# A hybrid gMLP and state-space block on one Trainium2 core: fixed places for the sums, the dt products and the modulation products of the first stage

## The chip, the cores and the metric

The kernel runs on one core of a Trainium2 chip. A core has five engines that run at the same time, each working through its own list of instructions in order: TensorE (PE in the profile) multiplies matrices, VectorE (DVE) and ScalarE (ACT) work element by element, GpSimd (POOL) does odd jobs, and SyncE (SP) mostly issues DMA transfers. An instruction that needs another engine's result waits on a semaphore, and everything behind it on its own engine waits with it. Operands lie in the on-chip memory SBUF, the results of matmuls in the accumulators of PSUM, which has eight banks; inputs and intermediate results too large for these lie in HBM.

The metric is the device time of one execution in microseconds (us), as the median of several runs. Lower is better.

## The reference, cut to what matters

One layer of a decoder trunk over a sequence of 1024 positions with width 1024. The first stage of the kernel computes `h` and its first products; the rest feeds on `h`.

```python
def hybrid_layer(x, c, ada_w, ada_b, norm_w, w_in, ...):
    mod = jax.nn.silu(c) @ ada_w + ada_b
    shift, scale, gate = jnp.split(mod, 3, axis=-1)
    h = rms_norm(x, norm_w) * (1 + scale[:, None, :]) + shift[:, None, :]
    proj = h @ w_in
    gm_u, gm_v, gm_z, ssm_z, xbc, dt_raw, g_a, g_b = jnp.split(proj, SPLITS, axis=-1)
    y_a = spatial_gating(gelu(gm_u), gelu(gm_v), gm_ln_w, gm_ln_b, gm_ws, gm_bs) * silu(gm_z)
    ...                       # causal convolution, state-space scan over 32 heads -> y_b
    merged = sigmoid(g_a) * (y_a @ w_proj_a) + sigmoid(g_b) * (y_b @ w_proj_b)
    return x + gate[:, None, :] * (merged @ w_out)

# reference(): x = hybrid_layer(x, c, ...); return rms_norm(x, final_norm_w)
```

`x` is 1024 x 1024, `w_in` is 1024 x 11296 and `ada_w` 1024 x 3072, all in float32.

## The kernel before, in words

The large products go through a scheme with seven products in place of eight: the 1024 x 1024 matrix `h`, transposed, is cut into quarters b11, b12 (upper row tiles, left and right half of the positions), b21 and b22 (lower row tiles), and besides b11, b21 and b22 the sums t1 to t4 of quarters are operands. To keep float32's accuracy with a faster matmul type, every operand is held as two parts, a rounded high part (written by ScalarE, `A.copy`) and the low part that is left (by VectorE, `V.tensor_sub`); a product then takes three matmuls: high by high, low by high, high by low.

The first stage makes all of this. Its loop runs over the eight row tiles of `h` (128 channels each) in the order `KS = (0, 4, 1, 5, 2, 6, 3, 7)`, so that a row tile k of the upper half and its partner k + 4 follow each other. With n as the place in this order, one row tile goes through these steps:

- SyncE loads a 1024 x 256 piece of `ada_w` (`load_aw`, two buffers, so the load for n + 2 waits for the product that reads n) and 128 x 256 of `w_in` (`load_w0`).
- `matvec(n)`: TensorE multiplies silu(c) by the piece of `ada_w`, eight matmuls into the bank `pm`; ScalarE copies the result to `row`.
- `modulation(n)`: two 128 x 1 matmuls turn the row into columns, again in `pm`, and VectorE makes the scale and shift `md` of the tile from them in two short instructions.
- `transposes(n, half)`: TensorE turns four 128 x 128 blocks of the already normed `x` into a bank `px`.
- `rows_of_h(n, half)`: from `px` and `md` ScalarE writes the rounded part and then the full value `hf`, and VectorE the low part. A tile has two halves, so four ScalarE instructions of 512 columns.
- `first_products(n)`: twelve matmuls, six for each half, add the tile's share of the first 256 gate columns into `acc`. Its generator gives the places, counted from 1 to 12, at which other work of the next tile is put: `prepare(n + 1)` holds what goes to which place.
- `dt_products(k)`: when both partners of k are there, four matmuls add their share of `dt_raw` into the bank `pd`. They read the full values `hf`.
- The sums: VectorE overwrites `hf` in four subtractions (the first makes b12 - b11 in the place of b11), which can only be done when `dt_products(k)` has read the values; then each of t1 to t4 is split into its two parts. For k = 0 to 2 this is `t_first`, `t_second`, `t_third` and `t_parts`; for k = 3 it is `last_sums` and what follows the stage.

Between these, at place 12 of tile n = 4, `small_parameters` transposes two blocks of small parameters into a bank `pp1` and VectorE copies them out in two instructions. `pp1` is allocated under the tag `pm`, which has one buffer: it is the bank that `matvec` and `modulation` use, and the next `matvec` may write there only when both copies are done. The diff does not touch `small_parameters`.

The order of instructions on an engine comes from a scheduler that sorts by its own estimate of when work is ready. An instruction wrapped in `pin` is held behind the instruction that the program wrote just before it on the same engine. A row of pinned instructions therefore keeps the program's order; an instruction without `pin` between them breaks the row, since it may itself go early or late, and what is pinned behind it is held behind nothing else. In the kernel before, matmuls and most work of the stage are pinned; the sums and splits of k = 0 to 2 are not. On VectorE the order that came out at tile n = 4 is: `md` of tile 5, the two copies of `small_parameters`, and then the low parts of tile 5's two halves, although the program writes the low parts first. Ahead of the loop, tiles n = 0 and the beginning of n = 1 are written out by hand, among `warm` matmuls that only keep TensorE running.

The first stage ends when the main stage's products begin (`vx` on line 944, whose first operand is `p1v0h`), and from there the kernel is one long row of matmuls with the other engines beside it.

Of the kernel before, what the change touches and what calls it, by code (L numbers as in the profile page):

```python
# [16 lines left out]
P = 128  # L17
D = 1024
S = 1024
KT = D // P  # L20
# [15 lines left out]
def hybrid_kernel(  # L36
# [131 lines left out]
    with tc.tile_pool(name="p0", bufs=1, reuse_waits="tile") as p0:  # L168
# [98 lines left out]

        def modulation(n):

            k, pm, row = KS[n], pms[n], mds[n]  # L270
            for j in range(2):
                mm(pm[:, 256 + j : 257 + j], row[:, j * P : (j + 1) * P], ones[:, 0:1])
# [33 lines left out]
        def t_split(nm, k, t):  # L306
            hi, lo = bop[nm][0][k], bop[nm][1][k]
            A.copy(hi, t)
            V.tensor_sub(lo, t, f32(hi))

        def t_first(k):

            b11, b12 = hfs[k, 0], hfs[k, 1]
            V.tensor_sub(b11, b12, b11)
            t_split("t1", k, b11)

        def t_second(k):

            b11, b12, b22 = hfs[k, 0], hfs[k, 1], hfs[k + 4, 1]
            V.tensor_sub(b12, b22, b12)  # L320
            V.tensor_sub(b22, b22, b11)

        def t_third(k):

            b21, b22 = hfs[k + 4, 0], hfs[k + 4, 1]
            V.tensor_sub(b21, b21, b22)
            t_split("t2", k, b22)

        def t_parts(k):

            t_split("t3", k, hfs[k, 1])
            t_split("t4", k, hfs[k + 4, 0])

        def last_sums(step):
            b11, b12, b21, b22 = hfs[3, 0], hfs[3, 1], hfs.get((7, 0)), hfs.get((7, 1))
            if step == 0:
                V.tensor_sub(b11, b12, b11)
# [62 lines left out]
        warm(2)  # L400
        modulation(0)
# [51 lines left out]
        sums = {(7, 9): [(last_sums, 0)], (7, 10): [(last_sums, 1)], (7, 11): [(last_sums, 2)]}  # L453
# [1469 lines left out]
```

## Time and profile before

| What | Value |
|---|---|
| Median of 3 runs | 1402.44 us (1399.79 to 1406.72) |
| The profiled execution's own time | 1400.27 us |
| Its span in the profile | 1398.5 us |
| Mean granted TensorE clock | 0.997 of full speed |
| First product of the main stage | 73.86 us from the span's start |

The profile shows one execution. Its views used below are: the page with busy time by engine and the chain of waits that ended last; windows, which give for stretches of time the busy time of each engine (with the number of instructions in brackets), the granted TensorE clock, the DMA share and GB/s; waits, which list who waited for whom; and the timeline, in which a row is the start and length of some merged instructions, their engine and line, what they write and read, how many, and in square brackets how long the engine had been idle before and what ended that. PEld is TensorE's loading of weights. A float32 matmul shows as two records, so eight matmuls of `matvec` are x16.

### The profile page before, as it was taken

Reading aid. Unit: us, or ns where it says so; the run is one execution under the profiler, and the core shown is the slowest. Engines: PE = TensorE matmul, PEld = TensorE weight load, DVE = VectorE, ACT = ScalarE, POOL = GpSimd, SP = SyncE. Lnnn points to the kernel's source line nnn. Section 1 sums busy time; section 2 is a strip of 40 time slices with the busy share of each in tenths; the row PEclk is TensorE's granted clock in tenths of the full one; section 3 lists DMA queues with packets and bytes.
Section 4 is the critical chain, followed back from the end, with each engine's and each line's share of the span. In section 5 each row is a group of like instructions: output and inputs, shape, how many; then the busy total and the mean of one; then the engine's idle time right before and its main releaser. Section 6 shows DMA issues by size and latency. Waiting matters only on the chain.

```text
span 1398.5 us, 20239 instructions
## 1 busy us (share of the span) xinstructions
PE 1366.6 (98%) x6959; PEld 1131.6 (81%) x6959; DVE 1047.8 (75%) x1701; ACT 800.1 (57%) x1447; POOL 221.7 (16%) x212
## 2 busy tenths in 40 slices
PE   7999999999999999999999999999999999999998
PEld 6678888888888888778888888888788888788886
DVE  4776876777778889688788786388777755859976
ACT  4754666666566665455666555587776713223453
POOL 1000000000000011121000110027778750000002
PEclk9999999999999999999999999999999999999999
DMA  9675443333334667686665775598778757978913
GB/s 266 172 244 143 141 120 116 103 121 113 121 121 147 199 192 242 217 255 204 215 199 169 237 235 151 174 349 308 270 257 289 254 184 248 351 252 318 369 69 121
DMA packets 247227, 288.60 MB, mean 206 GB/s; under 512 B 14508, under 2 KB 194132, under 8 KB 247124
## 3 DMA queue, kind: packets, MB, share of 16 engines
q1 hardware_dynamic: 173716, 203.76, 45.4%
q10 hardware_dynamic: 73408, 83.54, 17.5%
q8 instruction: 55, 0.90, 0.3%
q14 instruction: 48, 0.39, 0.1%
HBM read 199.79 MB, written 87.46 MB: 205 GB/s over the span
## 4 chain that ended last, share of the span: by engine, by line
PE 77%; DMA 8%; DVE 7%; ACT 3%; issue 3%; POOL 2%; SPq 1%; ACTq 0%; DVEq 0%; POOLq 0%
PE xuz L559 6%; PE xx L559 6%; PE xcb L559 5%; PE xz L559 5%; PE xg L559 4%; PE pma L81 3%; PE ox L1767 3%; DMA dcy<-acs_d 3%; PE yuz L559 3%; PE yp L1581 3%; PE vx L944 3%; PE yx L559 3%; PE ycb L559 3%; PE yz L559 3%; PE yg L559 2%
## 5 line engine op out<-in xcount | busy, mean ns | idle before, releaser
L782 POOL TENSOR_TENSOR wog<-wog,gb 128x256 f32<-128x256 f32 x16 | 21.6, 1366 | 628.3 <-DMA wog<-in_w_out_dram 604.1
L1102 ACT ACTIVATE dcy<-dcy,nacs 128x128 f32<-128x128 f32 x256 | 78.5, 388 | 15.2 <-POOL dcy L1097 15.1
L1097 POOL TENSOR_SCALAR_AFFINE_SELECT dcy<-dcy 128x1024 f32<-128x1024 f32 x32 | 35.4, 1107 | 137.2 <-ACT ea L1094 137.1
L1094 ACT ACTIVATE ea<-dcy 64x512 f32<-64x512 f32 x64 | 40.1, 626 | 12.4 <-DMA dcy<-acs_d 12.0
L1519 DVE SCALAR_TENSOR_TENSOR yn<-yn,par,rb 128x512 f32<-128x512 f32 x32 | 23.9, 747 | 27.0 <-DMA yn<-yb_d 26.9
L81 PE MATMUL pma<-yh,wah 128*128 128x512 f32 x128 | 43.3, 419 | 0.0
L81 PE MATMUL pma<-yh,wal 128*128 128x512 f32 x128 | 42.5, 413 | 0.0
L1122 DVE TENSOR_TENSOR dcy<-dcy,pc 128x1024 f32<-128x1024 f32 x32 | 38.9, 1216 | 4.7 <-PE pc L84 3.9
L1017 ACT ACTIVATE ac<-ac 128x1024 f32<-128x1024 f32 x32 | 33.9, 1061 | 13.6 <-DVE ac L1015 13.3
L1184 POOL TENSOR_TENSOR yz<-y,sl 128x512 f32<-128x512 f32 x32 | 41.5, 1296 | 1.1
L1182 DVE TENSOR_TENSOR ym<-yn,ea 128x512 f32<-128x512 f32 (+1 forms) x32 | 19.9, 622 | 28.7 <-PE yn L81 28.6
L81 PE MATMUL pma<-yl,wah 128*128 128x512 f32 x128 | 40.1, 394 | 0.0
L1183 POOL TENSOR_TENSOR y<-y,ym 128x512 f32<-128x512 f32 (+1 forms) x32 | 36.6, 1143 | 14.5 <-DVE ym L1182 14.0
L81 PEld LDWEIGHTS yn<-sl,st 128*128 128x128 f32 x224 | 30.7, 193 | 9.6 <-POOL yz L1184 3.6
L81 PE MATMUL yn<-sl,st 128*128 128x128 f32 x224 | 32.1, 279 | 6.1 <-DVE st L1152 6.1
L1782 POOL TENSOR_TENSOR r<-r,fnw 128x512 f32<-128x512 f32 x4 | 5.3, 1345 | 204.5 <-ACT junk L1780 204.5
L81 PE MATMUL sp<-xe,bn 128*128 128x256 f32 x112 | 32.6, 408 | 4.3 <-DVE ssq L1213 1.7
L814 ACT CAST wbb<-wbr 128x512 fp32r<-128x512 f32 x32 | 19.8, 620 | 28.8 <-DMA wb_d<-wbb 21.6
L1015 DVE SCALAR_TENSOR_TENSOR ac<-c2x,cwt,ac 128x1023 f32<-128x1023 f32 (+2 forms) x24 | 31.2, 1298 | 6.4 <-ACT ac L1013 6.3
L979 ACT ACTIVATE vm<-vm,vr 128x128 f32<-128x128 f32 x64 | 25.8, 483 | 16.2 <-DMA vm<-v_d 15.8
L1015 DVE SCALAR_TENSOR_TENSOR ac<-c2cb,cwt,ac 128x1023 f32<-128x1023 f32 (+2 forms) x24 | 31.2, 1299 | 5.2 <-ACT ac L1013 5.0
L81 PE MATMUL yi<-dcy,xd 128*64 128x128 f32 x512 | 35.0, 279 | 0.0
(2981 smaller groups left out, 4427.0 us busy)
## 6 DMA issues: line engine op xcount, KB each, us to landing
sl<-s_d SPq DMA_DIRECT2D x32, 768.0 KB
s_d<-ac ACTq DMA_DIRECT2D x32, 512.0 KB
wb_d<-wbb ACTq DMA_DIRECT2D x32, 512.0 KB
dcy<-acs_d SPq DMA_DIRECT2D x32, 512.0 KB
av<-in_w_in_dram SPq DMA_DIRECT2D x36, 256.0 KB
aw<-in_ada_w_dram SPq DMA_DIRECT2D x16, 512.0 KB
wbr<-in_w_proj_b_dram SPq DMA_DIRECT2D x32, 256.0 KB
yb_d<-yz ACTq DMA_DIRECT2D x32, 256.0 KB
```

Source lines behind the costliest of these rows:

```text
L81: pin(PE.matmul(acc, l, r, start=first, stop=last))
L559: pin(PE.matmul(ps, lw[:, k * P : (k + 1) * P], r[k], start=first and n + k == 0, stop=n == 2 and k == 3, skip_group_check=not first))
L944: pin(PE.matmul(ps[pn][j], l[:, j * P : (j + 1) * P], r, start=nm in ("p1", "p5", "p2") and n + units[i][1] == 0, stop=n == 2 and k == 3, ...
L1015: V.scalar_tensor_tensor(ac[:, s:], cc[:, : S - s], conv_wt[:, 3 - s, i : i + 1], ac[:, s:], op0=ALU.mult, op1=ALU.add)
L1094: A.activation(ea[hh * HD : (hh + 1) * HD], dcy.rearrange("p (j e) i l -> p e j (i l)", e=2)[hh * HD : (hh + 1) * HD, hh], AF.Exp)
L1097: G.affine_select(out=d8, in_=d8, compare_op=ALU.is_ge, fill=-1e30, base=0, pattern=[[0, 2 * HPG], [1, P]], channel_multiplier=-1)
L1102: A.activation(dcy[:, h, i, :], dcy[:, h, i, :], AF.Exp, bias=sub[:, i, h : h + 1])
L1122: V.tensor_tensor(d3, d3, pc[:, 0:256].unsqueeze(1).to_broadcast([P, HPG, 256]), op=ALU.mult)
L1183: G.tensor_add(y1[:, :, t0:], y1[:, :, t0:], m[:, :, t0:])
L1184: G.tensor_mul(yz, y1, sl[:, 4:6])
L1581: pin(PE.matmul(ps[j], a[:, v, js], r, start=first and n + k == 0, stop=n == 2 and k == KT - 1, skip_group_check=not first))
L1767: pin(PE.matmul(ps, a[:, tsl], b[:, cs], start=first and n + j == 0, stop=n == 2 and j == 3, skip_group_check=not first))
```

## The change

The diff moves work within the first stage. No computation is added or removed, except for four more `warm` matmuls.

- `modulation` is cut in two: `modulation_product` (the two 128 x 1 matmuls) and the two VectorE instructions. For tile 1 the written-out beginning now has the transposes and `rows_of_h(0, 1)` ahead of `matvec(1)`, and the product behind the first two matmuls of tile 0's second half; the split of `w_in`'s piece for tile 1 now stands ahead of VectorE's part of `modulation(1)`.
- The sums and splits of k = 0 to 2 are pinned and put at fixed places: `second` (the work at place 7, at place 8 for n = 2) and `between`.
- `dt_products` for k = 1 and 2 move from place 2 of the odd tile to the end of the transposes at place 7 of the same tile; for k = 3 from place 8 to place 6. `last_sums` for k = 3 moves from places 9, 10, 11 to 7, 8, 9, and its first sum is pinned.

```diff
-        def modulation(n):
-
-            k, pm, row = KS[n], pms[n], mds[n]
+        def modulation_product(n):
+
+            pm, row = pms[n], mds[n]
             for j in range(2):
                 mm(pm[:, 256 + j : 257 + j], row[:, j * P : (j + 1) * P], ones[:, 0:1])
+
+        def modulation(n):
+
+            k, pm = KS[n], pms[n]
             md = p0.tile([P, 2], F32, name=f"md{n}", tag="md", bufs=3)
...
         def t_split(nm, k, t):
             hi, lo = bop[nm][0][k], bop[nm][1][k]
-            A.copy(hi, t)
-            V.tensor_sub(lo, t, f32(hi))
...
+            pin(A.copy(hi, t))
+            pin(V.tensor_sub(lo, t, f32(hi)))
+
+        def t_sum(k, i):
+
+            b11, b12, b21, b22 = (hfs[k + 4 * (j // 2), j % 2] for j in range(4))
+            a, b, c = ((b11, b12, b11), (b12, b22, b12), (b22, b22, b11), (b21, b21, b22))[i]
+            pin(V.tensor_sub(a, b, c))
+
+        def t_part(k, nm):
+
+            t_split(nm, k, hfs[{"t1": (k, 0), "t3": (k, 1), "t2": (k + 4, 1), "t4": (k + 4, 0)}[nm]])
...
         start = first_products(0)
         for _ in range(6):
             next(start)
-        warm(6)
-        matvec(1)
+        warm(8)
         for t in (4, 5):
             normed(t, 1, V)
         transposes(0, 1)
+        rows_of_h(0, 1)
+        warm(2)
+        matvec(1)
+        split_w0(1)
+        for _ in range(2):
+            next(start)
+        modulation_product(1)
         modulation(1)
-        rows_of_h(0, 1)
-        split_w0(1)
         for t in (6, 7):
             normed(t, 1, V)
-        for _ in range(4):
-            next(start)
         rows_of_h(1, 0)
         for _ in start:
             pass
...
             a, b = halves(n)
+            k = (n - 2) // 2
+
+            def second():
+                modulation_product(n)
+                transposes(n, b)
+                if n % 2 == 0:
+                    dt_products(k)
+                modulation(n)
+                if n % 2:
+                    t_sum(k, 3)
+                rows_of_h(n, a)
+                if n % 2 == 0:
+                    t_sum(k, 0)
+                rows_of_h(n, b)
+                if n % 2:
+                    t_part(k, "t3")
+                    t_part(k, "t2")
+                else:
+                    t_sum(k, 1)
+
             if n == 2:
                 return {
                     4: lambda: (transposes(1, 1), rows_of_h(1, 1), matvec(n)),
-                    8: lambda: (transposes(n, a), modulation(n), transposes(n, b), rows_of_h(n, a), rows_of_h(n, b)),
+                    8: lambda: (transposes(n, a), second()),
                 }
-            return {
-                2: lambda: (matvec(n), transposes(n, a)),
-                7: lambda: (modulation(n), transposes(n, b), rows_of_h(n, a), rows_of_h(n, b)),
-            }
+            return {2: lambda: (matvec(n), transposes(n, a)), 7: second}
...
-        sums = {(7, 9): [(last_sums, 0)], (7, 10): [(last_sums, 1)], (7, 11): [(last_sums, 2)]}
-        sums |= {(5, 5): [(t_first, 2)], (5, 9): [(t_second, 2)], (6, 2): [(t_third, 2)], (6, 4): [(t_parts, 2)]}
...
-        for k in range(4):
-            sums[2 * k + 1, (8, 2, 2, 8)[k]] = [(dt_products, k)]
+        def between(n, at):
+
+            if n == KT - 1 and at in (6, 7, 8, 9):
+                (lambda: dt_products(3), *(lambda i=i: last_sums(i) for i in range(3)))[at - 6]()
+            elif at == 2 and n > 1:
+                k = (n - 2) // 2
+                if n % 2:
+                    t_part(k, "t4")
+                else:
+                    t_part(k, "t1")
+                    t_sum(k, 2)
```

On the engines, the built program of the changed kernel differs from the one before only in these first tiles, but for a few neighbours on VectorE and ScalarE that change places at the start of the main stage; SyncE's and GpSimd's orders are the same. Since the sums and splits are pinned now, VectorE's row of pinned work is unbroken, and its order at the same point is: `md` of tile 5, the last sum of k = 1, the low parts of tile 5's two halves, the low parts of t3 and t2 of k = 1, and then the two copies of `small_parameters`. On TensorE the order around them stays: the two transposes into `pp1`, the first two products of tile 5, `matvec(6)`.

More of the change, by code (lines that the diff above doesn't have):

```diff
@@ L336, in last_sums @@
             if step == 0:
-                V.tensor_sub(b11, b12, b11)
+                pin(V.tensor_sub(b11, b12, b11))
             elif step == 1:
@@ L400, in hybrid_kernel @@
         warm(2)
+        modulation_product(0)
         modulation(0)
@@ L450, in small_parameters @@
                 pin(V.tensor_copy(dskt[part, :], dsk.rearrange("p (i h) -> p i h", h=2)[part, :, hh]))
-        sums = {(7, 9): [(last_sums, 0)], (7, 10): [(last_sums, 1)], (7, 11): [(last_sums, 2)]}
-        sums |= {(5, 5): [(t_first, 2)], (5, 9): [(t_second, 2)], (6, 2): [(t_third, 2)], (6, 4): [(t_parts, 2)]}
-        for k in range(2):
-            sums[2 * k + 1, 5 if k else 9] = [(t_first, k)]
-            sums[2 * k + 1, 9 if k else 11] = [(t_second, k)]
-            sums[2 * k + 2, 5] = [(t_third, k)]
-            sums[2 * k + 2, 9] = [(t_parts, k)]
-        for k in range(4):
-            sums[2 * k + 1, (8, 2, 2, 8)[k]] = [(dt_products, k)]
+        def between(n, at):
[8 more added lines that the diff above has]
+                    t_sum(k, 2)
         for n in range(1, KT):
@@ L474, in hybrid_kernel @@
                     todo[at]()
-                for f, kk in sums.get((n, at), ()):
-                    f(kk)
                 if at == 2 and n < KT - 1:
                     split_w0(n + 1)
+                between(n, at)
                 if n == 4 and at == 12:
```

15 lines of the change are left out of this document (removed).

## The prediction

> **What bounds the kernel now.** I read the page first, for the engine that sets the end.
>
> ```profile
> span 1398.5 us, 20239 instructions
> PE 1366.6 (98%) x6959; PEld 1131.6 (81%) x6959; DVE 1047.8 (75%) x1701; ACT 800.1 (57%) x1447; POOL 221.7 (16%) x212
> PE 77%; DMA 8%; DVE 7%; ACT 3%; issue 3%; POOL 2%; SPq 1%; ACTq 0%; DVEq 0%; POOLq 0%
> ```
>
> TensorE is busy 98% of the span and has 77% of the chain that ended last. So a change in the first stage is worth what it does to the moment at which TensorE starts the main stage, unless the main stage has slack that swallows it. The windows answer that, and show the clock:
>
> ```profile
> 20.00:23.50 3.50, 1.15 (x11) 0.96 (x9) 2.35 (x7) 1.15 (x2) 1.21 (x2) 1.00 1.18 297
> 23.50:27.00 3.50, 2.95 (x22) 1.77 (x23) 0.35 (x1) 0.37 (x1) 0.00 (x0) 0.51 1.19 277
> 73.86:140.00 66.14, 66.03 (x290) 54.33 (x291) 47.78 (x81) 33.18 (x55) 0.00 (x0) 1.00 0.63 193
> ```
>
> Columns are the stretch, its length, busy time of PE, PEld, DVE, ACT, POOL, the granted clock, the DMA share and GB/s. From 73.86 on PE is busy 66.03 of 66.14 us, so a shift there is carried on one for one. In 20 to 23.5 PE worked 1.15 us of 3.5, and in the next 3.5 us its clock was 0.51.
>
> Next TensorE's waits between 18 and 75 us (total, times, longest), the most that the change can win there:
>
> ```profile
> PE pm L81 <- DMA aw<-in_ada_w_dram: 2.9, 1, 2.9
> PE acc L81 <- ACT b11h L299: 1.5, 2, 0.7
> PE vx L944 <- ACT p1v0h L874: 0.8, 1, 0.8
> PE acc L81 <- ACT b22h L299: 0.6, 1, 0.6
> ```
>
> They stand in TensorE's timeline. These are `matvec(1)`, the starts of the tiles n = 1, 3, 4, 5, 6 and 7, `matvec(4)` and `matvec(6)`, and the first product of the main stage:
>
> ```profile
> 24.05 1.93 PE L81 MATMUL pm<-aw,scz 128*32 128x256 f32 x16 [2.90 <-DMA aw<-in_ada_w_dram]
> ...
> 29.87 0.62 PE L81 MATMUL acc<-b21h,w0h 128*128 128x512 f32 x2
> ...
> 42.77 0.73 PE L81 MATMUL acc<-b22h,w0h 128*128 128x512 f32 x2 [0.65 <-ACT b22h L299]
> 43.43 1.07 PE L81 MATMUL pm<-aw,scz 128*32 128x256 f32 x16
> ...
> 50.18 0.73 PE L81 MATMUL acc<-b11h,w0h 128*128 128x512 f32 x2 [0.75 <-ACT b11h L299]
> ...
> 55.63 0.71 PE L81 MATMUL acc<-b22h,w0h 128*128 128x512 f32 x2
> 56.46 1.07 PE L81 MATMUL pm<-aw,scz 128*32 128x256 f32 x16
> ...
> 63.21 0.73 PE L81 MATMUL acc<-b11h,w0h 128*128 128x512 f32 x2 [0.74 <-ACT b11h L299]
> ...
> 68.53 0.61 PE L81 MATMUL acc<-b22h,w0h 128*128 128x512 f32 x2
> ...
> 73.86 0.73 PE L944 MATMUL vx<-p1v0h,b11h 128*128 128x512 f32 x2 [0.81 <-ACT p1v0h L874]
> ```
>
> The stage is TensorE's own work but for the load at its beginning and a wait of 0.65 to 0.81 us at four places. All that can be won is some 6 us of 1400.
>
> **The change part by part.** I follow the moment at which each tile starts.
>
> *The beginning.* The turns of tile 0's second half now go ahead of `matvec(1)`, which still waits for its load until 24.05. They need x scaled by VectorE:
>
> ```profile
> 22.58 1.28 DVE L381 TENSOR_SCALAR x<-x,rs 128x512 f32<-128x512 f32 x3 [0.43 <-POOL rs L374]
> 29.16 0.42 DVE L221 TENSOR_TENSOR w0l<-w0r,w0h 128x256 fp32r<-128x256 f32 x1
> ```
>
> The first of these three instructions is the last one needed, done near 23.0; the turns end near 23.3, and ScalarE writes the half in two steps to about 24.9, so it is ready in time. At 24.05 `matvec(1)` runs. If the clock stays full it takes 1.07 us (row at 43.43), not 1.93. I take it as full, since two more warm matmuls and the turns now fill part of the stretch that was busy to a third. Then the row copy, `w_in`'s high part and, on VectorE, its low part of 0.42 follow one another to about 26.5; only behind that low part comes `md` of tile 1, and then ScalarE's first part of the tile, 26.8 to 27.6. Tile 1 starts at 27.6 in place of 29.87: 2.2 us won; with a halved clock in `matvec(1)` and what follows it about 1.2 less. Four warm matmuls are added; they lie in the wait of 2.90 for the load. The load for tile 2 stays out of the way: behind tile 1's come 0.13 and 1.05 MB, 4.3 us at 277 GB/s, so it lands near 28.3, and `matvec(2)` is wanted at about 29.2.
>
> *The fixed places up to tile 5.* No sum or split is added, and TensorE's order keeps every instruction; the dt matmuls move between two places of one tile. With VectorE's sums no longer in front of them, `md` and the rows of the next tile come earlier, and the waits at 42.77 and 50.18 shrink. I take 0.4 of the first (one sum is still ahead of `md`) and all 0.75 of the second; bounds 0 and 1.4. Tile 5 starts 2.2 + 1.15 = 3.35 earlier, at 52.3.
>
> *The bank of the small parameters.* Here I expect the gain to go. `matvec(6)` writes the bank of `pp1` and must wait for VectorE's two copies out of it. Before, they came right behind `md` of tile 5, and this is what waited for their line:
>
> ```profile
> who waited for it (us, times):
>   PEld pm L81: 0.5, 1
> ```
>
> In the changed program they stand behind four subtractions: the low parts of tile 5's two halves and of t3 and t2. The second low part needs the last of ScalarE's four writes of the tile. First and last of these, the copies, and two neighbours among VectorE's 512-column subtractions:
>
> ```profile
> 54.42 0.78 ACT L299 ACTIVATE b22h<-px,md 128x512 fp32r<-128x512 f32 x1 [1.20 <-DVE md L275]
> ...
> 56.42 0.79 ACT L299 ACTIVATE hf<-px,md 128x512 f32<-128x512 f32 x1
> ```
>
> ```profile
> 55.92 0.29 DVE L447 COPY par<-pp 128x128 f32<-128x128 f32 x1 [1.59 <-PE pp L84]
> 56.12 0.28 DVE L447 COPY cwt<-pp 128x128 f32<-128x128 f32 x1
> ...
> 62.53 0.68 DVE L326 TENSOR_TENSOR hf<-hf 128x512 f32<-128x512 f32 x1
> 63.13 0.68 DVE L309 TENSOR_TENSOR t2l<-hf,t2h 128x512 fp32r<-128x512 f32 x1
> ```
>
> ScalarE's first write must be done when tile 5 starts, so it begins between 0.8 us ahead (its own length) and 1.2 (55.63 - 54.42); I take 0.9, 51.4. The last ends 56.42 + 0.79 - 54.42 = 2.8 later, at 54.2. Then VectorE: three subtractions at a step of 0.6, and copies of 0.2 and 0.3, to 56.5. TensorE is through tile 5's first two products at about 52.9 and stands until 56.5: 3.6 us (3.2 to 4.0). `matvec(6)` stood at 56.46 before, so the whole 3.35 is given back. Behind it on TensorE wait the turns, tile 5's other ten products and dt of k = 2; on ScalarE the row copy of tile 6, its split of `w_in` and t4's high part.
>
> *Tiles 5 to 7.* From `matvec(6)` to tile 6 took 63.21 - 56.46 = 6.75 with 0.74 of waiting at its end. The wait goes (bounds 0 and 0.9): tile 6 at 62.5, 0.7 won. Tile 6 to 7 took 5.32 without a wait; I add 0.2, since a sum now stands ahead of tile 7's `md`: 68.0, 0.5 won.
>
> *The end of the stage.* `p1v0h` stands on ScalarE behind t1's high part of k = 3, and that waits for the first of `last_sums` (line 337):
>
> ```profile
> 70.34 0.69 DVE L303 TENSOR_TENSOR b21l<-hf,b21h 128x512 fp32r<-128x512 f32 x1 [0.65 <-ACT hf L299]
> 71.95 0.69 DVE L337 TENSOR_TENSOR hf<-hf 128x512 f32<-128x512 f32 x1 [0.92 <-PE pd L81]
> 72.67 0.62 ACT L157 CAST t1h<-hf 128x512 fp32r<-128x512 f32 x1 [2.37 <-DVE hf L337]
> ```
>
> VectorE waited 0.92 for dt there. dt now comes two places earlier, but the low parts of t3, t2 and t4 of k = 2 are held ahead of that sum, three steps of 0.6. b21l moves with tile 7 to 69.8, so the sum starts at 69.8 + 0.6 + 1.8 = 72.2 against 71.95, and the main stage at 74.1: the 0.5 is lost and 0.25 more. TensorE's last wait grows from 0.81 to about 1.5.
>
> *The clock.* The new wait of 3.6 us is longer than that of 2.90 at 24.05, behind which the clock was 0.51 for about 3.5 us. TensorE will be busy under half of a stretch around it, so I expect one such drop between 55 and 60. It doubled `matvec` (1.93 for 1.07). Tile 5 has no slack for that: at most 3.5 / 2 = 1.75, less what of the drop falls into the standing itself. I take 1.5; bounds 0 and 3.3 (two drops).
>
> The Trainium skill, "TensorE: Matmul & The Clock Gate", section "Part 1: The HAM clock gate (the "warmup" mystery)", gives half rate only after at least one idle window of about 3.4 us, in windows that run freely. By that rule a wait of 3.6 us would seldom cover a whole window, and the sum would mostly be without this term. The first two windows above speak against it: a stretch busy to a third was enough.
>
> Sum: -3.35 at tile 5, +3.35 at `matvec(6)`, -0.7 + 0.2 + 0.75 to the main stage, +1.5 for the clock = +1.75 us. Against the profiled execution (1400.27: the span of 1398.5 and 1.8 around it) that is 1402.0. The median of the three runs lies 2.2 above that execution; the forecast is for a median, 1402.44 + 1.75 = 1404.2.
>
> **The rivals.** A difference of 0.5%, 7 us, is about what a measurement of this kernel can tell from no change; the three runs span 6.9.
>
> A: the clock stays full behind the stall. The places alone: +0.25, 1402.7. The windows above speak against it, 0.51 after 1.15 us of work. The rule cited would mostly give this.
>
> B: no stall at `matvec(6)`, and the change does at the places what their order suggests. Tile 6 then comes 3.35 + 0.7 earlier, 0.95 is lost to the end: -3.1, 1399.3. For it: the only wait for these copies was 0.5 us. Against: the order on VectorE, with ScalarE's writes and three subtractions ahead of them.
>
> C, slower: the clock halves for two windows at the stall, and still at the beginning. The place is a stall that splits evenly over two windows; the price 1.5 more there and 1.2 at the beginning: +4.45, 1406.9. It decides once both windows are busy under about a third to a half; at 3.6 us of standing that is just possible.
>
> D, much slower: the main stage's transfers, 8% of the chain or 112 us, fall otherwise after the shift and cost a sixteenth more, 7 us: 1411. Against: 0.11 us of idle in the 66 us behind the stage, and SyncE's order is the same.
>
> That the change doesn't do what it says is part of the forecast: its gain is there at tile 5 and gone at `matvec(6)`.
>
> **How the numbers follow.** Forecast 0.50, A 0.18, B 0.12, C 0.10, D 0.10. The forecast's own range, with about 2 us for a median of three, is 1401 to 1408. Leaving out no more than 2 in 10 takes in B and C with their spread on the far sides: 1398.5 to 1410. Slower by over 7 us (above 1409.5): D and some of C, 0.13. Faster by over 7 us (below 1395.4): B and a low draw, 0.05. The same: 0.82.
>
> **What would show it.** Right: TensorE idle 3.2 to 4.0 us ahead of `matvec(6)`, ended by VectorE's second copy; tile 1 at 27.6; no wait at tiles 4 and 6; a wait of about 1.5 at the main stage's first product, which starts at 74 to 77; a granted clock near a half in 55 to 61. Wrong: `matvec(6)` right behind tile 5's first products (B), a full clock there (A), or the main stage starting as forecast and the end over 5 us off (D).

## The result and the profile after

| | Before | Changed |
|---|---|---|
| Median of 20 runs each | 1400.54 us | 1404.95 us |
| Lowest and highest | 1395.53 and 1406.72 us | 1400.36 and 1410.08 us |
| Span of the profiled execution | 1398.5 us | 1402.3 us |
| First product of the main stage | 73.86 us | 76.29 us |

The ratio of changed to before is 1.0028, with a 95% interval from 1.0018 to 1.0038. That is 3.9 us slower (2.5 to 5.3; the medians differ by 4.4), less than the 0.5% that the prediction's chances call no change, but a slowdown. All ratios below are against the kernel before, which ran beside each group of experiments (medians 1400.37 to 1401.65). In three of the experiments (the small parameters two tiles later, warm matmuls in the stall, the last three splits) one execution took 3716 to 4125 us, and the ratios leave it out.

The first lines of the changed kernel's page, and TensorE's largest waits between 18 and 80 us (total, times, longest):

```profile
span 1402.3 us, 20248 instructions
PE 1370.3 (98%) x6967; PEld 1134.3 (81%) x6967; DVE 1047.3 (75%) x1701; ACT 800.8 (57%) x1447; POOL 221.6 (16%) x212
```

```profile
PE pm L81 <- DVE cwt L458: 3.6, 1, 3.6
PE vx L956 <- ACT p1v0h L886: 1.6, 1, 1.6
```

The span is 3.8 us longer and TensorE counts as busy for 3.7 us more (1370.3 for 1366.6), though it got only four small matmuls more. A matmul at the half clock counts as busy for nearly twice as long (`matvec` 1.94 us for 1.07), so a busy sum that grows with the span already hints at the clock. The waits before were of 2.9 us for a load and of 0.6 to 0.8 us at four places; now one of 3.6 us for VectorE's second copy of the small parameters leads.

TensorE's timeline of the changed kernel, in its rows for the starts of the tiles n = 1, 3, 4 and 5, `matvec(6)`, the tiles 6 and 7, and the main stage's first product:

```profile
27.24 0.73 PE L81 MATMUL acc<-b21h,w0h 128*128 128x512 f32 x2 [0.15 <-ACT b21h L303]
...
39.63 0.73 PE L81 MATMUL acc<-b22h,w0h 128*128 128x512 f32 x2
...
46.22 0.63 PE L81 MATMUL acc<-b11h,w0h 128*128 128x512 f32 x2
...
51.62 0.74 PE L81 MATMUL acc<-b22h,w0h 128*128 128x512 f32 x2
...
55.95 1.94 PE L81 MATMUL pm<-aw,scz 128*32 128x256 f32 x16 [3.60 <-DVE cwt L458]
...
64.59 0.61 PE L81 MATMUL acc<-b11h,w0h 128*128 128x512 f32 x2
...
69.97 0.73 PE L81 MATMUL acc<-b22h,w0h 128*128 128x512 f32 x2
...
76.29 0.73 PE L956 MATMUL vx<-p1v0h,b11h 128*128 128x512 f32 x2 [1.60 <-ACT p1v0h L886]
```

Up to tile 5 the kernel is ahead of before, by 2.6 us at tile 1 and by 4.0 at tile 5 (51.62 against 55.63). At `matvec(6)` 0.5 of that is left, at tile 6 it is 1.4 us behind, and at the main stage 2.4. The waits in brackets at tiles 3, 4 and 6 are gone.

VectorE's timeline there shows what the 3.6 us wait for. The brackets hold VectorE's own idle time:

```profile
52.27 0.69 DVE L307 TENSOR_TENSOR b22l<-hf,b22h 128x512 fp32r<-128x512 f32 x1 [0.98 <-ACT hf L303]
53.60 0.69 DVE L307 TENSOR_TENSOR b21l<-hf,b21h 128x512 fp32r<-128x512 f32 x1 [0.65 <-ACT hf L303]
54.21 0.68 DVE L313 TENSOR_TENSOR t3l<-hf,t3h 128x512 fp32r<-128x512 f32 x1
54.81 0.69 DVE L313 TENSOR_TENSOR t2l<-hf,t2h 128x512 fp32r<-128x512 f32 x1
55.41 0.28 DVE L458 COPY par<-pp 128x128 f32<-128x128 f32 x1
55.62 0.28 DVE L458 COPY cwt<-pp 128x128 f32<-128x128 f32 x1
```

The copies come behind the four subtractions, the first two of which wait for ScalarE. The clock is read from windows that are laid on the edges at which it changed (columns as in the prediction's windows; the second number is PE's busy time, the third from the end the granted clock):

```profile
51.75:55.16 3.41, 0.60 (x3) 0.16 (x2) 2.25 (x4) 2.85 (x5) 0.00 (x0) 1.00 0.46 140
55.16:58.57 3.41, 2.62 (x20) 1.36 (x21) 0.98 (x5) 0.56 (x2) 0.00 (x0) 0.50 0.00 0
58.57:61.99 3.42, 3.42 (x13) 2.94 (x12) 1.36 (x4) 0.63 (x2) 0.00 (x0) 0.50 0.26 77
```

The half clock lasted for two stretches of 3.41 us, not one. It begins at the end of a stretch in which PE worked 0.60 us, and it goes on after a stretch in which PE was busy for 2.62 us.

### The profile page after: what moved, and what is told of

Same layout as the page of the kernel before. It is cut to its first block, busy times and chain, and to the rows that moved or that the text cites. A ratio compares the mean times of both kernels' runs of the same rounds, so it can differ in the third digit from the quotient of the medians.

```text
span 1402.3 us, 20248 instructions
## 1 busy us (share of the span) xinstructions
PE 1370.3 (98%) x6967; PEld 1134.3 (81%) x6967; DVE 1047.3 (75%) x1701; ACT 800.8 (57%) x1447; POOL 221.6 (16%) x212
## 4 chain that ended last, share of the span: by engine, by line
PE 71%; DMA 9%; DVE 7%; ACT 5%; issue 3%; POOL 2%; SPq 1%; ACTq 0%; DVEq 0%; POOLq 0%
PE xuz L571 6%; PE xx L571 5%; PE xcb L571 5%; PE xz L571 5%; PE xg L571 5%; PE ox L1779 3%; PE yp L1593 3%; PE pma L81 3%; PE vx L956 3%; PE yuz L571 3%; PE ycb L571 3%; PE yx L571 3%; PE yz L571 3%; DMA dcy<-acs_d 2%; PE yg L571 2%
```

## The experiments

The theory at the start was this. The stall at `matvec(6)`, which comes from the place of two short copies in VectorE's order, gives back what the beginning and the fixed places win, and the half clock behind it makes the loss. The rivals were that the places themselves cost the time, that the main stage swallows or adds several microseconds whatever the first stage does, and that the end of tile 7, where three splits now stand ahead of the last sums, decides.

### The small parameters two tiles later

```diff
-                if n == 4 and at == 12:
+                if n == 6 and at == 12:
                     small_parameters()
```

> The changed kernel with small_parameters moved from place 12 of tile 4 to place 12 of tile 6, behind the last use of the bank pm. Theory (the bank of the small parameters and the halved clock behind it cost what the places win): no wait at matvec(6), which starts near 52.5, a full clock from 20 us on, tile 6 near 58.2, and the main stage starts at 70 to 71 instead of 76.29 (73.86 before): about 5.5 us faster than the changed kernel, ratio to the kernel before about 0.9975. Rival (the extra time sits in the main stage, where a few neighbours changed places and loads fall otherwise): the main stage starts as early, but the time is not under that of the kernel before, ratio 1.000 or above.

Ratio 0.9995 (0.998 to 1.001). TensorE's timeline of this kernel, in the rows for `matvec(6)`, tile 6 and the main stage:

```profile
52.49 1.07 PE L81 MATMUL pm<-aw,scz 128*32 128x256 f32 x16
...
58.43 0.63 PE L81 MATMUL acc<-b11h,w0h 128*128 128x512 f32 x2
...
70.92 0.73 PE L956 MATMUL vx<-p1v0h,b11h 128*128 128x512 f32 x2 [2.39 <-ACT p1v0h L886]
```

The stall is gone, `matvec(6)` runs at the full clock (1.07 us), and the main stage starts 5.4 us ahead of the changed kernel. The ratio is 0.0033 below the changed kernel's, 4.6 us of 1400, but the time is no better than before, although the main stage starts 2.9 us before the 73.86 of its profile. One reason stands in this execution's windows: a stretch at the half clock lies right behind the wait of 2.39 us at the main stage's start.

```profile
72.30:75.71 3.41, 3.41 (x10) 2.50 (x9) 3.41 (x7) 3.41 (x8) 0.00 (x0) 0.50 0.70 217
```

Two more such stretches follow near 1127 and 1188 us; the table behind the experiments comes back to them.

### The old beginning with the new places

The written-out beginning (lines 405 to 418 of the changed kernel) is put back as it was before; the rest stays as changed.

```diff
-        warm(8)
+        warm(6)
+        matvec(1)
...
-        rows_of_h(0, 1)
-        warm(2)
-        matvec(1)
-        split_w0(1)
...
+        rows_of_h(0, 1)
+        split_w0(1)
```

> The changed kernel with the written-out beginning of before (matvec(1) ahead of the turns, six warm matmuls). Theory (a shift of the first tiles is carried through to the end): tile 1 starts at 29.9 again instead of 27.24, with a clock near a half in 23.5 to 27, the stall at matvec(6) is again 3.6, and the main stage starts 2.3 to 2.8 later than in the changed kernel, near 78.8: ratio to the kernel before about 1.0045. Rival (the shift is swallowed by the stall or behind it): ratio 1.0028 as for the changed kernel.

Ratio 1.0037 (1.0024 to 1.0049). Timeline, `matvec(1)`, `matvec(6)` and the main stage, and the windows on the clock's edges around the stall:

```profile
24.13 1.07 PE L81 MATMUL pm<-aw,scz 128*32 128x256 f32 x16 [1.77 <-DMA aw<-in_ada_w_dram]
...
57.21 1.81 PE L81 MATMUL pm<-aw,scz 128*32 128x256 f32 x16 [3.62 <-DVE cwt L457]
...
76.35 0.73 PE L955 MATMUL vx<-p1v0h,b11h 128*128 128x512 f32 x2 [1.60 <-ACT p1v0h L885]
```

```profile
53.97:57.38 3.41, 0.17 (x4) 0.16 (x8) 2.75 (x8) 1.89 (x4) 0.00 (x0) 1.00 0.14 43
57.38:60.80 3.42, 3.42 (x23) 2.08 (x16) 0.91 (x3) 1.20 (x3) 0.00 (x0) 0.50 0.19 40
```

The stall is the same 3.6 us without the new beginning, so it comes from the fixed places. Here it lies almost wholly in one stretch (PE busy 0.17 us), and only one stretch at half clock follows. The main stage therefore starts as late as in the changed kernel (76.35 and 76.29), although `matvec(6)` comes 1.3 us later. The slowdown is at least as large as the changed kernel's: the new beginning does not cause it. The half clock that was expected in 23.5 to 27 us did not come: `matvec(1)` takes 1.07 us, behind a wait for its load of 1.77 us. This and the one stretch fewer behind the stall are why the main stage does not start as late as the 78.8 that was expected.

### Warm matmuls in the stall

Thirteen warm matmuls go into the stall, between tile 5's first two products and `matvec(6)`. They write the bank `px` of the next turn, which the turn then overwrites. The copies stay where they are.

```diff
+        def filled(n, h):
+            pxs[n, h] = px = ax(f"px{n}_{h}", "px")
+            for _ in range(13):
+                mm(px[:, 0:P], ident, ones)
...
+            if n == 6:
+                return {2: lambda: (filled(n, a), matvec(n), transposes(n, a)), 7: second}
```

> The changed kernel with 13 warm matmuls (128 columns, into the bank that the next turns overwrite) ahead of matvec(6), so that TensorE works through the stall; its result is unchanged. Theory (the halved clock behind the stall costs 2.8 us: matvec(6) to tile 6 took 8.64 us, matvec(4) to tile 4 took 5.86): matvec(6) still starts near 56, the clock is full in 55 to 62, tile 6 starts near 61.8 instead of 64.59 and the main stage near 73.5, ratio to the kernel before 1.000 to 1.001. Rival (what is slow behind the stall is the pile-up of VectorE and ScalarE, not the clock): tile 6 at 64 to 65 and the ratio stays at 1.0028.

Ratio 0.9996 (0.9982 to 1.001). Timeline: `matvec(1)`, the warm matmuls, `matvec(6)`, tile 6 and the main stage:

```profile
25.47 1.93 PE L81 MATMUL pm<-aw,scz 128*32 128x256 f32 x16
...
55.31 3.17 PE L81 MATMUL px<-ones,ident 128*128 128x128 f32 x26
...
58.98 1.07 PE L81 MATMUL pm<-aw,scz 128*32 128x256 f32 x16 [0.50 <-DVE cwt L465]
...
64.82 0.62 PE L81 MATMUL acc<-b11h,w0h 128*128 128x512 f32 x2
...
76.52 0.73 PE L963 MATMUL vx<-p1v0h,b11h 128*128 128x512 f32 x2 [1.60 <-ACT p1v0h L893]
```

This is the run that separates the wait from the clock. TensorE still cannot start `matvec(6)` before the second copy, but the clock stays full, and from `matvec(6)` to tile 6 it takes 64.82 - 58.98 = 5.84 us, against 64.59 - 55.95 = 8.64 in the changed kernel. So the half clock costs 2.80 us there. The times agree with that: with the warm matmuls the slowdown is gone. The wait alone only gives back what was won. The profile itself starts late for another reason: in this execution the half clock fell on the beginning, with `matvec(1)` at 25.47 taking 1.93 us.

### The last three splits out of tile 7

The splits of t2, t3 and t4 of k = 2 move from tile 7 into the main stage's first products (`u` counts these).

```diff
-                if n % 2:
+                if n % 2 and k < 2:
                     t_part(k, "t3")
                     t_part(k, "t2")
...
                 last_split("t3")
+                t_part(2, "t2")
...
+                t_part(2, "t3")
+            elif u == 3:
+                t_part(2, "t4")
```

> The changed kernel with the splits of t2, t3 and t4 of k = 2 moved from ahead of last_sums into the first products of the main stage. Theory (three low parts on VectorE hold up the sum that the main stage's first operand waits behind): the wait ahead of the main stage falls from 1.60 to 0.3 to 0.8, it starts near 75.2, ratio to the kernel before about 1.002. Rival (VectorE is full at that point, so its work only moves): the main stage starts earlier, but TensorE then waits for low parts among its first 40 products, and the ratio stays at 1.0028 or grows.

Ratio 1.0032 (1.0014 to 1.005). Timeline: the first product of the main stage and one 5.7 us later:

```profile
74.00 0.73 PE L957 MATMUL vx<-p1v0h,b11h 128*128 128x512 f32 x2 [0.36 <-ACT p1v0h L887]
...
79.66 0.74 PE L957 MATMUL vx<-p1v0h,b11h 128*128 128x512 f32 x1 [2.00 <-ACT sg L509]
```

The wait ahead of the main stage shrinks from 1.60 to 0.36 us, as it should if the splits in front of the last sums set it. But a wait of 2.00 us for ScalarE stands 5.7 us later instead. The splits were not free anywhere; moved all together, they only take the wait along. The clock has a part in both places. Behind the stall, `matvec(6)` still waits 3.60 us, but the half clock lasts one stretch in this execution (55.86 to 59.27) and not two, so that the main stage starts ahead of the 75.2 that was expected. Another such stretch stands behind the wait of 2.00 us:

```profile
79.75:83.16 3.41, 3.41 (x8) 2.67 (x9) 2.61 (x5) 2.95 (x6) 0.00 (x0) 0.50 0.81 286
```

### The new beginning alone

The kernel before with the changed kernel's written-out beginning and nothing else of the change.

```diff
-        warm(6)
-        matvec(1)
+        warm(8)
...
+        warm(2)
+        matvec(1)
         split_w0(1)
+        for _ in range(2):
+            next(start)
+        modulation_product(1)
+        modulation(1, False)
```

> The kernel before with the new written-out beginning alone; the sums, dt's products and modulation products stay at the places of before, and every later instruction keeps its order. Theory (a gain of the first stage is carried to the end as long as nothing halves the clock behind it): tile 1 at 27.3 us instead of 29.8, no wait of 3.6 us at matvec(6), the main stage at 71.3 to 71.7 instead of 73.86, ratio 0.998 to 0.9985. Rival 1 (the main stage swallows 2 to 3 us of shift, since it waits for transfers and VectorE at fixed points): main stage at 71.5 all the same, but a ratio of 0.9995 to 1.0005. Rival 2 (the clock's window at 20 to 23.5 us is not tripped, but a later one is): ratio 1.000 to 1.002 with a halved window that the kernel before does not have.

Ratio 0.9993 (0.998 to 1.0007). Timeline of this kernel, `matvec(1)`, tile 1 and the main stage:

```profile
24.34 1.07 PE L81 MATMUL pm<-aw,scz 128*32 128x256 f32 x16
...
27.69 0.74 PE L81 MATMUL acc<-b21h,w0h 128*128 128x512 f32 x2 [0.15 <-ACT b21h L305]
...
71.81 0.73 PE L952 MATMUL vx<-p1v0h,b11h 128*128 128x512 f32 x2 [0.81 <-ACT p1v0h L882]
```

Tile 1 is where it should be, and the main stage starts 2.05 us ahead of the first profile of before, but the ratio says 1.0 us, and its interval includes no gain at all. The next run shows a reason.

### A second profile of the kernel before

> The kernel before, unchanged, profiled a second time. The half rate came in stretches of 3.41 us on a grid whose place in the kernel differs from one profile to the next. Theory (whether a short pause halves the clock depends on where that grid lies): the stretch at 23.5 to 26.9 us of the first profile need not be there; if it is not, matvec(1) takes 1.07 us instead of 1.93 and the main stage starts 1.5 to 2 us earlier, at 72 to 72.4. Rival (the half rate at the beginning belongs to the kernel before): matvec(1) takes 1.9 us again and the main stage starts at 73.7 to 74.

Its one execution took 1398.67 us. Timeline (`matvec(1)`, tile 1, the main stage) and the window around the wait for the load. It lies on the clock's grid, 294 steps of 3.413 us ahead of this profile's half-clock stretch that begins at 1026.17:

```profile
24.29 1.07 PE L81 MATMUL pm<-aw,scz 128*32 128x256 f32 x16 [2.29 <-DMA aw<-in_ada_w_dram]
...
28.79 0.62 PE L81 MATMUL acc<-b21h,w0h 128*128 128x512 f32 x2
...
72.78 0.73 PE L944 MATMUL vx<-p1v0h,b11h 128*128 128x512 f32 x2 [0.81 <-ACT p1v0h L874]
```

```profile
22.65:26.07 3.42, 1.78 (x22) 1.15 (x23) 1.28 (x3) 0.45 (x2) 0.13 (x1) 1.00 1.10 284
```

The half clock at 23.5 us, on which a part of the prediction rests, was a matter of that one profile. Here the wait for the same load is 2.29 us instead of 2.90, the stretch around it has 1.78 us of work in it, and the clock stays full, as it did behind the wait of 1.77 us in the run with the old beginning. The main stage starts at 72.78, 1.08 earlier. Against this profile the new beginning wins 72.78 - 71.81 = 0.97 us, which is what its ratio says (0.0007 of 1401 is 1.0, though the interval reaches from a loss of 1.0 to a gain of 2.8). And the changed kernel's main stage starts 76.29 - 72.78 = 3.5 us late, which is nearly all of its 3.9; against the first profile it is 2.4.

### A second profile of the changed kernel

> The changed kernel, unchanged, profiled and timed a second time beside the kernel with the copies not held. Theory: the wait at matvec(6) is as long as a stretch of the clock's grid, so the half rate follows it in every profile, for one stretch or two by where the grid lies; matvec(6) to tile 6 takes 7 to 8.7 us, the main stage starts at 74.6 to 76.4, ratio 1.002 to 1.004. Rival (the half rate after the wait was this one profile's): matvec(6) to tile 6 takes 5.9 us, main stage at 73.5.

Ratio 1.0023 (1.0009 to 1.0037). Timeline, `matvec(6)`, tile 6 and the main stage:

```profile
55.96 1.94 PE L81 MATMUL pm<-aw,scz 128*32 128x256 f32 x16 [3.60 <-DVE cwt L458]
...
64.44 0.62 PE L81 MATMUL acc<-b11h,w0h 128*128 128x512 f32 x2
...
76.14 0.74 PE L956 MATMUL vx<-p1v0h,b11h 128*128 128x512 f32 x2 [1.59 <-ACT p1v0h L886]
```

Wait, half clock and late start come back: 64.44 - 55.96 = 8.48 us from `matvec(6)` to tile 6. Unlike the drop at the beginning of before, this one was in both profiles of the changed kernel, and in those of both other kernels that keep the stall empty.

### The two copies not held

One word of the changed kernel: the copies out of `pp1` are no longer held behind the instruction written before them.

```diff
-                pin(V.tensor_copy((par2, cwt)[i], pp[:, i * P : (i + 1) * P]))
+                V.tensor_copy((par2, cwt)[i], pp[:, i * P : (i + 1) * P])
```

In the built order the copies then stand ahead of tile 5's two low parts, as before the change. The scheduler also puts some instructions near 1185 us (`p1bl`, `yn` and their neighbours on VectorE and ScalarE) in another order than in the two original kernels. So a second version has one warm matmul less ahead of `matvec(1)`, with which that late order is the original one.

> The changed kernel with the two copies of pp1 no longer held behind t2l on VectorE: in the built order they go ahead of b22l, as in the kernel before. The build also moves two instructions past each other near 1185 us (p1bl and yn), which the changed kernel and the kernel before have in one order. Theory: matvec(6) starts at 52.3 to 52.7 without a wait and at the full clock, tile 6 at 58.4, the main stage at 70.5 to 71 behind a wait of 1.6 to 2.4 us. What the time makes of it: 0.997 to 0.9985 if the first stage's 3 us are kept; 0.9995 to 1.0005 if the other order near 1185 us or the main stage takes them back, as in the run with the parameters in tile 6. Rival (the stall moves to another wait of the same tile, t2l and par being late for something else): main stage at 73 or later, ratio 1.000 to 1.002.

> As the run with the copies not held, with one warm matmul less ahead of matvec(1) (0.1 us), by which the build leaves the instructions near 1185 us in the order of before. Theory (the other order there is what cost the run with the parameters in tile 6 its gain): the same first stage as the run beside it, main stage at 70.5 to 71, but no wait of 3 us at 1187 us, and a ratio of 0.997 to 0.9985, 0.1 to 0.2% below the run beside it. Rival (the main stage swallows the shift whatever that order is): the two agree within 0.1%, both at 0.999 to 1.0005.

> The changed kernel with the two copies of pp1 not held and one warm matmul less, a second time. Theory (it beats both kernels, by the 3 us of the first stage of which 1 is lost later): main stage at 70 to 71, ratio 0.9975 to 0.9990, and 0.4% below the changed kernel beside it. Rival (its first ratio of 0.9983 was the draw of few executions, its like with the late instructions in the other order being at 0.9992): ratio 0.9992 to 1.0002.

Ratios: 0.9992 (0.9977 to 1.0007) with the other late order, 0.9983 (0.9973 to 0.9994) and, the second time, 0.9992 (0.9978 to 1.0006) with the original one. Timelines of the first and of the second version (`matvec(6)`, the main stage, and the row near 1185 us):

```profile
52.73 1.07 PE L81 MATMUL pm<-aw,scz 128*32 128x256 f32 x16
...
70.27 0.73 PE L956 MATMUL vx<-p1v0h,b11h 128*128 128x512 f32 x2 [1.60 <-ACT p1v0h L886]
...
1186.11 0.62 PE L1593 MATMUL y3p<-p3bh,p3a 128*128 128x512 f32 x1 [3.01 <-DVE tri L1239]
```

```profile
52.66 1.07 PE L81 MATMUL pm<-aw,scz 128*32 128x256 f32 x16
...
70.22 0.73 PE L956 MATMUL vx<-p1v0h,b11h 128*128 128x512 f32 x2 [1.60 <-ACT p1v0h L886]
...
1181.52 0.50 PE L1593 MATMUL y3p<-p3bh,p3a 128*128 128x512 f32 x1 [1.27 <-DVE tri L1239]
```

With that one word the stall and the half clock are gone, and the main stage starts 6.1 us before the changed kernel's and 2.6 us before that of the second profile of before. The late order was suspected of the loss near 1185 us, and the two profiles look like it, but the timings do not settle it: the second run with the original order gave the same 0.9992 as the other order. The table below takes it up again.

### Parameters early and the tail spread out

The transposes into `pp1` and the copies are made in tile 2; of the last three splits t3 goes to tile 6, and t2 and t4 into the main stage's products, one by one.

```diff
+                if n == 2:
+                    first_parameters()
...
+                    if k == 2:
+                        t_part(k, "t3")
...
+            elif u in (3, 4):
+                t_part(2, ("t2", "t4")[u - 3])
```

> The changed kernel with pp1's transposes and copies in tile 2 and the last three splits of k=2 taken out of tile 7: t3 in tile 6, t2 and t4 in the main stage's products. Theory: no stall at matvec(6), main stage at 69 to 69.7 behind a wait below 1 us, ratio 0.9965 to 0.998. Rival (as in the run with all three splits in the main stage's first products: ScalarE and VectorE are full there, and t2 and t4 make the products wait): the start is as early, but 1 to 4 us are lost within the first 40 us of the main stage, ratio 0.999 to 1.002.

Ratio 0.9985 (0.9971 to 1.0). The timeline has the main stage where it was expected:

```profile
69.68 0.74 PE L963 MATMUL vx<-p1v0h,b11h 128*128 128x512 f32 x2 [0.35 <-ACT p1v0h L893]
```

Spread out, the splits bring the start 0.54 us ahead of that with the copies not held (70.22), and the wait ahead of it down to 0.35. In the time that cannot be seen.

### What the main stage does with an earlier start

Each span less the start of its main stage, from the rows above and the spans of the pages:

| Kernel | Main stage starts | Span | From there to the end | Half-clock stretches |
|---|---|---|---|---|
| before, first and second profile | 73.86, 72.78 | 1398.5, 1397.0 | 1324.6, 1324.2 | 1, 1 |
| changed, first and second profile | 76.29, 76.14 | 1402.3, 1405.7 | 1326.0, 1329.6 | 1, 3 |
| old beginning, new places | 76.35 | 1404.6 | 1328.3 | 2 |
| warm matmuls in the stall | 76.52 | 1404.1 | 1327.6 | 2 |
| new beginning alone | 71.81 | 1401.1 | 1329.3 | 2 |
| copies not held, original late order, twice | 70.22, 70.59 | 1394.8, 1396.5 | 1324.6, 1325.9 | 0, 2 |
| copies not held, other late order | 70.27 | 1400.3 | 1330.0 | 2 |
| parameters two tiles later, other late order | 70.92 | 1401.8 | 1330.9 | 3 |
| parameters early, tail spread, other late order | 69.68 | 1398.1 | 1328.4 | 1 |

The last column counts the stretches of 3.41 us at the half clock between the main stage's start and 1390 us. The kernel with the three splits moved together is left out, since it makes a new wait of its own in the main stage.

The same kernel takes 1326.0 and 1329.6 us here in two profiles. So a difference of 3 us in the main stage between two single profiles shows nothing about a change to the first stage; only the many timed runs do. Across the table an earlier start is neither kept better nor worse than a late one: 1324.6 stands beside both 73.86 and 70.22. The times go rather with the half clock: with none or one such stretch they are 1324.2 to 1326.0 us but for the last row's 1328.4, with two or three 1325.9 to 1330.9. At half the rate a stretch of 3.41 us costs 1.7 us at most, so a part of these differences must lie in the waits ahead of the stretches. The timed runs agree: in the 88 executions of before that ran beside the experiments, 0.001 less of mean granted clock goes with 1.0 us more (correlation -0.78), in the 32 of the changed kernel with 1.6 us (-0.82).

The three with the other late order lie at the upper end (1328.4 to 1330.9), but the changed kernel and the new beginning alone get to 1329.6 and 1329.3 with the original order. The long wait near 1185 us does not need that order either. These are its rows in the first and the second profile of the changed kernel:

```profile
1189.26 0.50 PE L1593 MATMUL y3p<-p3bh,p3a 128*128 128x512 f32 x1 [1.29 <-DVE tri L1239]
```

```profile
1191.61 0.79 PE L1593 MATMUL y3p<-p3bh,p3a 128*128 128x512 f32 x1 [3.48 <-DVE tri L1239]
```

The order is the same in both. VectorE, which TensorE waits for, had stood there for the load of `yn` from `yb_d`, 4.18 us in the first and 6.78 in the second. Whether the other order costs anything stays open.

## Why the prediction came out as it did

**The chain of steps held.** The forecast was 1404.2 us, the measured median 1404.95. The gain up to tile 5, its loss at the bank of the small parameters, and a loss behind it through the clock are all in the profile. The experiments show them to be causes: with the copies ahead of the low parts, or the parameters elsewhere, stall and slowdown go.

**The stall.** Forecast 3.6 us, ended by the second copy; measured 3.60, ended by the second copy. The row for `matvec(6)` is 55.95 for 56.5. That came from counting what stands ahead of the copies in the changed order. No row of the profile before showed a wait of this size there; it had to be built from ScalarE's four writes and three steps of VectorE.

**The places.** Tile 5 was forecast 3.35 us earlier and came 4.0 earlier: both waits, at tiles 3 and 4, went whole (0.65 and 0.75), and tile 1 came at 27.24 for 27.6. Tile 6 to 7 took 5.38 for 5.5, the last wait grew to 1.60 for 1.5.

**The clock was the step that failed in size.** The term in the sum was +1.5 us, one stretch at half clock; measured it is 8.64 - 5.84 = 2.80, inside its bounds of 0 to 3.3 but nearly twice the value taken. The drop lasted two stretches. Rival C had two drops, but on the condition that the stall splits evenly and both stretches are busy under about a third to a half. The second stretch was busy for 2.62 of 3.41 us, so that condition was wrong: after a half-clock stretch that was busy to three quarters, the half clock stayed.

The Trainium skill, "TensorE: Matmul & The Clock Gate", section "Part 1: The HAM clock gate (the "warmup" mystery)", gives the half rate after at least one idle window of about 3.4 us. The measurement differs: 0.60 us of work stood in the stretch before the drop. Its statement that the windows run freely agrees with the traces, whose stretches lie elsewhere from one profile to the next (the first drop of the changed kernel begins at 55.16 us in one and at 54.81 in the other).

**The beginning was over-valued.** The prediction took 2.2 us for tile 1 and named 1.2 of it as dependent on the clock. The second profile of before shows that its half clock at 23.5 us need not be there: then tile 1 starts at 28.79 and the main stage at 72.78. With the full clock in both, the new beginning alone starts the main stage 0.97 us earlier; against an execution of before with the half clock there it is 2.05. Of three profiles with the old beginning one has that half clock, and of ten with the new one also one: in the run with warm matmuls in the stall, `matvec(1)` took 1.93 us. The timed ratio alone (0.998 to 1.0007) would allow the 2.2 as well.

**Two errors in opposite directions.** The median of three runs to which the sum was added, 1402.44, lay 1.9 us above the median of twenty (1400.54). The forecast difference of +1.75 was 2.7 us too small against the medians' 4.41 (2.2 against the 3.9 of the ratio); the clock, 1.3 too small, and the beginning, about 1.2 too large, account for most of it. The forecast time is only 0.8 us off because 1.9 and 2.7 partly cancel, and that is luck. The difference, not the time, is what the reasons should be held against.

**The rivals.** A (clock full): no; both profiles of the changed kernel have the half clock. B (no stall) was -3.1 us; the kernel that makes it true, with the copies not held, gives 0.9983 and 0.9992, that is 2.4 and 1.1 us faster, since the beginning is worth less than thought: its main stage starts at 70.22, 3.6 us before that of the first profile of before but only 2.6 before the second's. C's price of two drops at the stall came true, without a drop at the beginning. D (transfers fall otherwise, 7 us): the main stage added 1.4 and 5.0 us against the first profile of before in the two profiles of the changed kernel, but these go with one and with three half-clock stretches there (the table). Of the 3.9 us that were timed the late start explains 3.5 against the second profile of before and 2.4 against the first, so 0.4 to 1.5 is left for the main stage, and nothing like 7.

**A version ahead of both.** The changed kernel with the copies not held and one warm matmul less is 0.31% below the changed kernel beside it in its second run (0.9992 against 1.0023). Against before, the two runs weighted by their intervals give 0.9986; with the intervals taken as independent that is 0.9978 to 0.9995, about 2 us of gain. The whole difference to the changed kernel hangs on the place of two copies.

## What to carry to other kernels

When a row of instructions is fixed in order, look for the short instructions that used to slip ahead and free something, here a PSUM bank by two copies of 0.28 us; ask of each what it frees and who waits for it. Price a stall of TensorE by what the clock does behind it as well as by its length: filling it with useless matmuls took back the 2.8 us behind a wait that itself stayed. And before building on a row of a profile that has the half clock in it, take a second profile; here it halved what the new beginning seemed to win at the main stage (2.05 us against the first profile, 0.97 against the second).

## What the runs showed of the hardware

- The half clock came in stretches of 3.41 us. Within a profile they begin a whole number of steps of 3.413 us apart (55.16 and 1031.37 us in the changed kernel, 286 steps; 55.86 and 79.75 with the three splits moved, 7 steps). Where the steps lie shifts from profile to profile (54.81 in the changed kernel's second).
- No idle stretch is needed: PE worked 0.60 us in the stretch before the drop in the changed kernel. In the first profile of before the wait for the load was 2.90 us, less than a stretch, and PE worked 1.03 us in the one before the drop:

```profile
20.12:23.53 3.41, 1.03 (x10) 0.84 (x8) 2.38 (x7) 1.15 (x2) 1.09 (x2) 1.00 1.19 297
```

- The same load's waits of 2.29 us (second profile of before) and 1.77 us (old beginning, new places) did not trip it. There the wait is shorter and lies elsewhere on the grid; these profiles don't tell which of the two decides.
- How long PE was busy in a stretch does not decide alone. After 1.76 us (22.0 to 25.4 with the warm matmuls) the clock halved, after 1.78 in the second profile of before it did not, and after 2.01 (1126.6 to 1130.0 in the changed kernel's second profile) it did.
- Recovery also depends on how busy a stretch is. After half-clock stretches with PE busy for 2.62 us (changed kernel) and 2.25 (its second profile) of 3.41 the half clock stayed for a second one; after 2.89 (first profile of before), 2.91 (three splits moved) and 3.42 (old beginning) it ended. No profile has a half-clock stretch between 2.62 and 2.89.
